# Where eight blocks of weight digits are made: all ahead of the pooling groups, two to every three gate steps

## The chip, the cores and the metric

The kernel runs on one core of one Trainium2 chip. The metric is the device time of one execution in microseconds (us). Before the change three executions took 1553.84, 1555.45 and 1555.94 us, a median of 1555.45 us. One more execution was profiled. It took 1551.45 us, and its span from the first to the last instruction is 1549.5 us.

The engines are named as in the profile: PE is the matrix engine and PEld its weight load, DVE the vector engine, ACT the scalar engine, POOL the GpSimd engine, SP the engine that issues most DMAs. Each takes its instructions strictly in the order in which they stand in its queue, so an instruction that waits holds up all that stand behind it.

## The reference: what is computed

One encoder layer on 1024 tokens of 1024 channels, all in float32:

```python
h = rmsnorm(x, g_mix[l])
z = h @ w_in[l]
...
y_pool = pool_mixer(u_pool, w_pool_grp[l], pool_scale[l])
...
y_attn = diff_attention(q, k, v, g_q[l], g_k[l], lam, g_sub[l], lambda_init)

gates = jax.nn.sigmoid(h @ w_gate[l] + b_gate[l])
merged = (gates[..., :D_MODEL] * (y_pool @ w_branch_pool[l])
          + gates[..., D_MODEL:] * (y_attn @ w_branch_attn[l]))
x = x + merged @ w_out[l]
h2 = rmsnorm(x, g_ffn[l])
x = x + jnp.square(jax.nn.relu(h2 @ w_up[l])) @ w_down[l]
```

The attention has eight heads with two softmax maps each. The pooling mixer has four groups of 128 channels with trailing windows of 2, 4, 8 and 16 tokens. The change touches how `w_branch_attn` is prepared for the product `y_attn @ w_branch_attn`.

## The kernel before, in words

**Products.** Every float32 product is made of three products of reduced parts (`mm3`, lines 125 to 127): a number is split into a high part, which ACT rounds (L119), and a low part, the rest, which DVE or POOL subtracts (L120). Most PE time is in these three lines.

**The attention stage** works through 8 heads of 8 token tiles each, 64 steps, as a pipeline whose stages lie some steps apart (`O`): A projects a tile to q, k and v (tile `z`), B scales them (`ms`, `qn`), C transposes (`tk`), D makes scores and softmax (`sc`, `s`), E transposes the probabilities (`ta`), F multiplies with the values (`po`), H and R make the norms (`SS`, `r`, `trr`). The weights of the next head are loaded and split during the last steps of a head; POOL makes their low parts (`wqkv`). POOL also makes every power (`ms`, L234) and scales `qn` (L433). The last tile of a head has the longest rows of probabilities, 1024 wide, and needs the most of DVE.

**The filling work.** Behind this pipeline in the program, but meant to run in its gaps on PE, stands work that the attention doesn't need:

- *Gate steps* (`gate_step`). `gates()` yields 32 steps, half a column of gate weights each: 24 matmuls of 512 columns into tile `g`, one ACT instruction (`go`, L731) and a store to DRAM. The weights of a column are loaded (L657) and split, the low part by POOL (`fwgate`). 13 gate steps come first (`G_FIRST`).
- *Four pooling groups* (`pool_group(0)` to `(3)`). For each half of the tokens: 24 matmuls (`u`), an ACT copy into tile `u` (L696), 1, 2, 3 or 4 shifted additions on DVE (L705), a scaled difference (L714), a split (`mix`), a gate step, and three matmuls (`yp`). So each group holds two gate steps.
- *Eight units of weight digits* (`weight_unit`, called by `prepare_weights`). The attention branch uses a fast matrix product with seven combinations of blocks of `w_branch_attn`. A unit loads a block (tile `wq`, two DMAs, L753), and POOL makes from it seven pairs of digits: seven roundings (L762), seven subtractions (L763), four sums or differences (L767, L779). SP stores each pair to DRAM (`wa_dram`, L764, seven DMAs). POOL alone computes here; PE, DVE and ACT take no part.

**Shared room.** A unit's block `wq` lies in the same buffer as the groups' `mix` (tag `mx`), and its digits `wd` in the same buffer as the groups' `u` (tag `fu`), and there is one of each. So a group's copy into `u` can't be made before the stores of the unit that holds the buffer have finished, and the other way round. PSUM has one bank for the filling work (`ps_f`, `N_F` = 1): while `u` waits there to be copied, no gate step can begin. Later gate steps (`G_Z` = 13 and on) take turns with the two banks of `z` as well.

**Where the units stand.** `gate_step` counts the steps, and after the steps numbered in `PREP_AT` a unit follows: before the change at steps 3, 5, 7, 9 and 12. The other three stand after the groups 0, 1 and 2. A unit may not be issued before the low part of the last weights that were split (`tc.issue_after(stored["lo"])`).

**The order.** Nobody writes the order of the queues by hand. A scheduler takes the instructions by their place in the program as a priority, and by its own estimate of when each can run, and places the filling work in the gaps of the attention that it expects. On the chip the queues are then fixed.

**After the attention stage** the remaining gate steps run, then the pooling branch (`bp`), for which `ypT` is loaded and split and whose weights `wbp` POOL splits, then the attention branch (`baX`, `baY`), which loads the digits back (`wa`, L876) and needs the norm factors that go through `r` (POOL, L594 and L595), `trr` (PE, L597) and DRAM. Then come the output projection and the MLP.

Of the kernel before, what the change touches and what calls it, by code (L numbers as in the profile page):

```python
# [36 lines left out]
N_YU = 5  # L37
N_QKVW = 8 * H
N_AHEAD_B, N_AHEAD_A = 5, 3
PREP_AT = (3, 5, 7, 9, 12)  # L40


START = "x0 g n0 w0 w1 w2u w3u x1 s0p s1 x2 s2p s3 x3"
# [14 lines left out]
def encoder_kernel(  # L58
# [688 lines left out]
    def weight_unit(src, digits, kk, ch):  # L747

        cs = slice(ch * 256, (ch + 1) * 256)
        q = fq.tile([P, 4, 256], F32, tag="mx", name=f"wq{kk}_{ch}")  # L750
        for i in range(2):
            r0 = (kk + 4 * i) * P
            nc.sync.dma_start(  # L753
                q[:, i::2, :], src[r0 : r0 + P, :].rearrange("p (i c) -> p i c", i=2)[:, :, cs]
            )
        a11, a12, a21, a22 = (q[:, i, :] for i in range(4))
        buf = fu_tile(f"wd{kk}_{ch}").rearrange("p (s h c) -> p s h c", s=2, h=2)

        def put(j, a):
            d = buf[:, nput[0] % 2]  # L760
            nput[0] += 1
            nc.gpsimd.tensor_copy(d[:, 0, :].bitcast(F32R), a)  # L762
            nc.gpsimd.tensor_tensor(d[:, 1, :].bitcast(F32R), a, d[:, 0, :], op=ALU.subtract)  # L763
            nc.sync.dma_start(digits[ORDER_BA.index((j, kk))][:, :, cs], d)  # L764

        def minus(o, x_, y_):
            nc.gpsimd.tensor_tensor(o, x_, y_, op=ALU.subtract)  # L767

        nput = [0]
        put("1", a11)  # L770
        minus(a21, a11, a21)
        put("7", a21)
        put("2", a12)
        minus(a21, a22, a21)
        put("6", a21)
        put("4", a22)
        minus(a12, a12, a21)
        put("3", a12)
        nc.gpsimd.tensor_tensor(a11, a11, a21, op=ALU.add)  # L779
        put("5", a11)  # L780
# [5 lines left out]
    def gate_step():  # L786
        more = next(gate_units, "end") != "end"
        steps[0] += 1
        if steps[0] in PREP_AT:
            prepare_weights()  # L790
        return more

    def prepare_weights():
        with tc.issue_after(stored["lo"]):
            weight_unit(w_branch_attn, wa_dram, *units_left.pop(0))
# [3 lines left out]
    for g in range(4):  # L799
        for _ in pool_group(g):  # L800
            gate_step()
        if g < 3:
            prepare_weights()
    while gate_step():
        pass
    assert not units_left
# [648 lines left out]
```

## Time and profile before

| what | value |
|---|---|
| median of three executions | 1555.45 us |
| the profiled execution, its own time | 1551.45 us |
| its span | 1549.5 us |
| PE busy | 1519.3 us, 98% of the span |
| DVE busy | 1052.1 us, 68% |
| ACT busy | 814.5 us, 53% |
| POOL busy | 361.0 us, 23% |
| clock granted to PE | 1.00 |

The profiled execution is 4.0 us below the median of the others. The attention stage lies between about 15 and 690 us of the span, the branch products end at about 840, the MLP takes the rest. In the windows below, a stretch's length less its PE busy time is the time in which PE had nothing running; matmuls are pipelined, so a matmul's own duration is longer than the distance to the next one.

### The profile page before, as it was taken

The numbers are of one execution on the slowest core, as the hardware profiler recorded it, in microseconds if no ns is written. First come the engines' busy times: TensorE is split into PE (matmuls) and PEld (weight loads), VectorE is DVE, ScalarE is ACT, GpSimd is POOL, SyncE is SP. The second block draws the span as 40 slices with busy tenths as digits, with TensorE's granted clock in tenths as the row PEclk, the third lists the DMA queues.
The fourth block names the chain that finished last, engine by engine and source line by source line (L and its number), as shares of the span: only waits on it lengthen the run. The fifth ranks groups of instructions, "written<-read, shape, count | busy, mean of one in ns | idle before, by whom it ended". The sixth has DMA issues, their size and how long they took to land.

```text
span 1549.5 us, 22331 instructions
## 1 busy us (share of the span) xinstructions
PE 1519.3 (98%) x7601; PEld 1309.8 (85%) x7601; DVE 1052.1 (68%) x2349; ACT 814.5 (53%) x1808; POOL 361.0 (23%) x536
## 2 busy tenths in 40 slices
PE   7999999999999999999999999999999999999998
PEld 6999999989889899788888887888888788888887
DVE  6777777777877787843568648766666668556672
ACT  6666565556565655544454556556555634333331
POOL 6666572434636373312000000000000000000000
PEclk9999999999999999999999999999999999999999
DMA  7343331111213141627675733555443789537650
GB/s 243 119 128 102 99 110 42 56 54 62 89 40 126 37 137 48 213 76 237 249 258 178 264 109 121 182 170 181 134 139 109 254 310 397 193 123 249 230 193 27
DMA packets 183275, 235.80 MB, mean 152 GB/s; under 512 B 11685, under 2 KB 114810, under 8 KB 183162
## 3 DMA queue, kind: packets, MB, share of 16 engines
q1 hardware_dynamic: 165754, 207.08, 40.3%
q10 hardware_dynamic: 17408, 27.30, 4.7%
q8 instruction: 60, 0.98, 0.3%
q14 instruction: 53, 0.43, 0.1%
HBM read 165.10 MB, written 69.24 MB: 151 GB/s over the span
## 4 chain that ended last, share of the span: by engine, by line
PE 84%; DVE 6%; DMA 3%; issue 3%; ACT 2%; SPq 1%; POOL 0%; POOLq 0%; ACTq 0%; DVEq 0%
PE z L125 5%; PE z L127 5%; PE z L126 5%; PE Da L126 4%; PE Da L127 4%; PE Da L125 4%; PE g L125 3%; PE g L126 3%; PE g L127 3%; PE Db L126 3%; PE Db L127 3%; PE Db L125 3%; PE X L125 2%; PE X L127 2%; PE X L126 2%
## 5 line engine op out<-in xcount | busy, mean ns | idle before, releaser
L125 PE MATMUL z<-wqkv,hT 128*128 128x384 f32 x512 | 174.7, 342 | 0.8 <-DVE qn L427 0.7
L127 PE MATMUL z<-wqkv,hT 128*128 128x384 f32 x512 | 173.3, 339 | 0.0
L126 PE MATMUL z<-wqkv,hT 128*128 128x384 f32 x512 | 173.1, 339 | 0.0
L496 ACT ACTIVATE s<-s,nm 128x256 f32<-128x256 f32 (+7 forms) x128 | 99.7, 779 | 70.9 <-DVE nm L488 67.0
L125 PE MATMUL g<-hT,fwgate 128*128 128x512 f32 x256 | 101.0, 394 | 0.7 <-ACT go L731 0.5
L125 PEld LDWEIGHTS z<-wqkv,hT 128*128 128x128 f32 x512 | 96.5, 188 | 5.1 <-DVE qn L427 2.5
L126 PE MATMUL g<-hT,fwgate 128*128 128x512 f32 x256 | 100.7, 393 | 0.0
L127 PE MATMUL g<-hT,fwgate 128*128 128x512 f32 x256 | 100.2, 393 | 0.0
L126 PEld LDWEIGHTS z<-wqkv,hT 128*128 128x128 f32 x512 | 96.5, 189 | 2.7 <-POOL wqkv L120 0.2
L127 PEld LDWEIGHTS z<-wqkv,hT 128*128 128x128 f32 x512 | 96.3, 188 | 2.5 <-DVE hT L120 0.7
L234 POOL TENSOR_TENSOR ms<-ms,mhalf 128x4 f32<-128x4 f32 x64 | 67.0, 1046 | 96.2 <-DVE ms L233 79.4
L488 DVE CUSTOM_DVE_ANT_0 s<-sc,dist 128x512 f32<-128x512 f32 (+3 forms) x128 | 74.6, 584 | 17.6 <-PE sc L486 16.1
L485 PE MATMUL sc<-K,Q 128*128 128x512 f32 (+2 forms) x192 | 67.5, 361 | 2.1 <-DVE nm L488 1.9
L120 DVE TENSOR_TENSOR AS<-s,AS 128x512 fp32r<-128x512 f32 x64 | 43.8, 687 | 35.5 <-ACT AS L119 35.3
L486 PE MATMUL sc<-K,Q 128*128 128x512 f32 (+2 forms) x192 | 66.0, 354 | 0.0
L120 POOL TENSOR_TENSOR wqkv<-rqkv,wqkv 128x384 fp32r<-128x384 f32 x60 | 63.2, 1068 | 11.8 <-ACT wqkv L119 8.5
L459 ACT CAST Q<-tk 64x128 fp32r<-64x128 f32 x128 | 33.2, 260 | 61.1 <-DVE Q L458 58.8
L120 POOL TENSOR_TENSOR fwgate<-frgate,fwgate 128x512 fp32r<-128x512 f32 x32 | 43.4, 1361 | 87.4 <-ACT fwgate L119 78.8
L456 ACT CAST Q<-tk 64x128 fp32r<-64x128 f32 x128 | 33.0, 258 | 44.9 <-DVE K L455 43.5
L125 PEld LDWEIGHTS g<-hT,fwgate 128*128 128x128 f32 x256 | 48.1, 188 | 9.9 <-ACT go L731 1.1
L127 PEld LDWEIGHTS g<-hT,fwgate 128*128 128x128 f32 x256 | 48.0, 188 | 8.7
L126 PEld LDWEIGHTS g<-hT,fwgate 128*128 128x128 f32 x256 | 48.1, 188 | 8.0
(460 smaller groups left out, 4652.7 us busy)
## 6 DMA issues: line engine op xcount, KB each, us to landing
wd<-in_w_down_dram SPq DMA_DIRECT2D x56, 512.0 KB, 5.6
wu<-in_w_up_dram SPq DMA_DIRECT2D x32, 512.0 KB, 4.8
udS<-us SPq DMA_DIRECT2D x64, 256.0 KB, 2.7
ur<-udS SPq DMA_DIRECT2D x32, 512.0 KB, 3.4
wa_dram<-wd SPq DMA_DIRECT2D x56, 256.0 KB, 2.8
wa<-wa_dram SPq DMA_DIRECT2D x28, 512.0 KB, 6.5
rqkv<-in_w_in_dram SPq DMA_DIRECT2D x64, 192.0 KB, 2.7
ud<-u ACTq DMA_DIRECT2D x48, 256.0 KB, 2.1
```

Source lines behind the costliest of these rows:

```text
L120: return (lo_eng or nc.vector).tensor_tensor(lo, src, f(hi), op=ALU.subtract)
L125: nc.tensor.matmul(ps, lhs_hi, rhs_hi, start=first, stop=False, **kw)
L126: nc.tensor.matmul(ps, lhs_hi, rhs_lo, start=False, stop=False, **kw)
L127: nc.tensor.matmul(ps, lhs_lo, rhs_hi, start=False, stop=last, **kw)
L234: nc.gpsimd.tensor_tensor(dst, dst, mhalf[:, :n], op=ALU.pow)
L456: nc.scalar.copy(q_hi, q)
L459: nc.scalar.copy(Q[other, m, 1, :], q)
L485: nc.tensor.matmul(dst, Q[:, i, 0, :], rhs, start=True, stop=False)
L486: nc.tensor.matmul(dst, Q[:, i, 1, :], rhs, start=False, stop=True)
L488: nc.vector.tensor_tensor_reduce(out=s[i][:, c : c + w], in0=sc[:, 0:w], in1=dist[:, o0 + c : o0 + c + w], scale=2.0 ** -(h + 1), scalar=B ...
L496: nc.scalar.activation(s[i][:, 0:n], s[i][:, 0:n], AF.Exp, bias=last, scale=-1.0, accum_out=Z[:, i, t : t + 1])
```

## The change

All eight units now follow gate steps: two to every three steps, after the steps 2, 3, 5, 6, 8, 9, 11 and 12. None is left between the groups. Nothing is computed otherwise; the number of instructions of each kind stays.

```diff
-PREP_AT = (3, 5, 7, 9, 12)
+PREP_AT = (2, 3, 5, 6, 8, 9, 11, 12)
...
     for g in range(4):
         for _ in pool_group(g):
             gate_step()
-        if g < 3:
-            prepare_weights()
     while gate_step():
         pass
```

The scheduler makes new queues from this. Three places of them follow.

The first is SP's queue around the loads of group 1. `frpool` and `rgrp` are loads of a pooling group's weights, `frgate` of a gate column's, `rqkv` of the next head's, `wq` is the load of a unit and `wa_dram<-wd` are its stores. Before:

```order
L657 DMA frpool_1_7914<-in_w_in_dram 128x4x128
L690 DMA rgrp_7919<-in_w_pool_grp_dram 128x128
L657 DMA frgate_0_8034<-in_w_gate_dram 128x4x128
L753 DMA wq_1_7880<-in_w_branch_attn_dram 128x2x256 x2
L657 DMA frgate_1_8039<-in_w_gate_dram 128x4x128
L764 DMA wa_dram<-wd_1_7883 256x1x256
L308 DMA rqkv_2_4224<-in_w_in_dram 128x3x128 x2
L308 DMA rqkv_3_4233<-in_w_in_dram 128x3x128 x2
L764 DMA wa_dram<-wd_1_7883 256x1x256
L308 DMA rqkv_0_5045<-in_w_in_dram 128x3x128 x2
L308 DMA rqkv_1_5054<-in_w_in_dram 128x3x128 x2
L764 DMA wa_dram<-wd_1_7883 256x1x256 x5
```

The same group's loads in SP's queue after the change:

```order
L657 DMA frpool_0_7967<-in_w_in_dram 128x4x128
L657 DMA frpool_1_7972<-in_w_in_dram 128x4x128
L690 DMA rgrp_7977<-in_w_pool_grp_dram 128x128
L657 DMA frgate_0_8092<-in_w_gate_dram 128x4x128
L657 DMA frgate_1_8097<-in_w_gate_dram 128x4x128
L308 DMA rqkv_2_4224<-in_w_in_dram 128x3x128 x2
L308 DMA rqkv_3_4233<-in_w_in_dram 128x3x128 x2
L308 DMA rqkv_0_5045<-in_w_in_dram 128x3x128 x2
L308 DMA rqkv_1_5054<-in_w_in_dram 128x3x128 x2
```

The load and the seven stores of the sixth unit have left this place, and now stand ahead of the loads of group 0. Those of the seventh and the eighth, which stood at the groups 2 and 3, now stand among the loads of group 0 and end ahead of those of group 1.

The second place is DVE's queue at the end of head 5 (the sixth of eight). `s_7` and `cf_7` belong to its last tile, `rz` marks its norms; `sum` and `mix` are group 2's first half. Before:

```order
L705 TENSOR_TENSOR sum_0_4_8156<-sum_0_2_8153 128x508
L457 TENSOR_TENSOR Q_0_5432<-tk_0_5429,Q_0_5432 64x128
L458 TENSOR_TENSOR Q_0_5432<-tk_0_5429,Q_0_5432 64x128
L711 TENSOR_TENSOR sum_0_4_8156<-sum_0_4_8156,inv 128x7
L714 SCALAR_TENSOR_TENSOR sum_0_4_8156<-sum_0_4_8156,u_8123 128x505
L712 TENSOR_TENSOR sum_0_4_8156<-sum_0_4_8156,u_8123 128x7
L590 RECIPROCAL rz_5846<-Z_4423 128x8
L455 TENSOR_TENSOR K_0_5258<-tk_0_5429,K_0_5258 64x128
L120 TENSOR_TENSOR AT_3_0l<-ta_6_0_5458,AT_3_0h 128x4x128
L488 ISA s_7_1_5446,nm_7_5447<-sc_7_1_0_5481,dist 128x512
L488 ISA nm_7_5447 128x1
L120 TENSOR_TENSOR mix_0_8162<-sum_0_4_8156,mix_0_8162 128x512
```

The same place after the change:

```order
L457 TENSOR_TENSOR Q_0_5432<-tk_0_5429,Q_0_5432 64x128
L458 TENSOR_TENSOR Q_0_5432<-tk_0_5429,Q_0_5432 64x128
L590 RECIPROCAL rz_5846<-Z_4423 128x8
L455 TENSOR_TENSOR K_0_5258<-tk_0_5429,K_0_5258 64x128
L120 TENSOR_TENSOR AT_3_0l<-ta_6_0_5458,AT_3_0h 128x4x128
L120 TENSOR_TENSOR oqs_2_5517<-oq_2_5513,oqs_2_5517 128x256
L457 TENSOR_TENSOR Q_0_5432<-tk_0_5429,Q_0_5432 64x128
L458 TENSOR_TENSOR Q_0_5432<-tk_0_5429,Q_0_5432 64x128
L488 ISA s_7_1_5446,nm_7_5447<-sc_7_1_0_5481,dist 128x512
L488 ISA nm_7_5447 128x1
```

Group 2's first half has moved out of the end of head 5, to the middle of the head, and its second half begins nine rows behind the last tile's L505. Group 3's second half, which stood in the last head, now stands at the end of head 6, where its first half stood.

The third place is POOL's queue at the end of the attention stage. `fwgate` are the last gate columns, `wbp` weights of the pooling branch, `r` the norm factors of the last head, which `trr` on PE waits for. Before:

```order
L120 TENSOR_TENSOR fwgate_0_8761<-frgate_0_8759,fwgate_0_8761 128x512
L120 TENSOR_TENSOR fwgate_1_8766<-frgate_1_8764,fwgate_1_8766 128x512
L594 TENSOR_TENSOR r_7119<-r_7119,mhalf 128x8
L595 TENSOR_TENSOR r_7119<-r_7119,rz_7118 128x8
L120 TENSOR_TENSOR wbp_0_8942<-rbp_8940,wbp_0_8942 128x512
L120 TENSOR_TENSOR wbp_1_8945<-rbp_8940,wbp_1_8945 128x512
L120 TENSOR_TENSOR wbp_0_9038<-rbp_9036,wbp_0_9038 128x512
```

After the change:

```order
L120 TENSOR_TENSOR fwgate_0_8761<-frgate_0_8759,fwgate_0_8761 128x512
L120 TENSOR_TENSOR fwgate_1_8766<-frgate_1_8764,fwgate_1_8766 128x512
L120 TENSOR_TENSOR wbp_0_8942<-rbp_8940,wbp_0_8942 128x512
L120 TENSOR_TENSOR wbp_1_8945<-rbp_8940,wbp_1_8945 128x512
L594 TENSOR_TENSOR r_7119<-r_7119,mhalf 128x8
L120 TENSOR_TENSOR wbp_0_9038<-rbp_9036,wbp_0_9038 128x512
L595 TENSOR_TENSOR r_7119<-r_7119,rz_7118 128x8
```

The last head's factors now stand behind three splits of the pooling branch's weights. On PE, `trr` stood 43 gate matmuls ahead of the first `bp`; it now stands behind the first 23 matmuls of `bp`. And of the filling matmuls (`g`, `u`, `yp`) 295 stood behind the beginning of the last `z` tile before, and 242 do now: the scheduler has placed 53 more of them among the heads before.

## The prediction

> **What bounds the kernel now.** I read the page first, then the waits of PE, then windows around each stretch in which PE had nothing running. The page:
>
> ```profile
> span 1549.5 us, 22331 instructions
> ...
> PE 1519.3 (98%) x7601; PEld 1309.8 (85%) x7601; DVE 1052.1 (68%) x2349; ACT 814.5 (53%) x1808; POOL 361.0 (23%) x536
> ...
> PE   7999999999999999999999999999999999999998
> ...
> POOL 6666572434636373312000000000000000000000
> ...
> PE 84%; DVE 6%; DMA 3%; issue 3%; ACT 2%; SPq 1%; POOL 0%; POOLq 0%; ACTq 0%; DVEq 0%
> ```
>
> PE is busy 98% of the span and holds 84% of the chain that ended last. The change takes no matmul away, so it can only gain or lose in PE's gaps, 1549.5 - 1519.3 = 30.2 us in all. POOL, which makes the units, works in the first half only and is on that chain with 0%. A unit costs POOL this (columns: nanoseconds shortest/median/longest):
>
> ```profile
> L762 POOL CAST wd<-wq x56: 388/398/1171, 43.6 to 580.6; 128x256 fp32r<-128x256 f32 x56
> L763 POOL TENSOR_TENSOR wd<-wq,wd x56: 724/737/1612, 44.7 to 581.4; 128x256 fp32r<-128x256 f32 x56
> L767 POOL TENSOR_TENSOR wq<-wq x24: 722/737/1290, 35.8 to 573.5; 128x256 f32<-128x256 f32 x24
> ...
> L779 POOL TENSOR_TENSOR wq<-wq x8: 729/739/741, 47.0 to 572.4; 128x256 f32<-128x256 f32 x8
> ```
>
> Seven of the first, seven of the second, three and one of the others: 7 x 0.398 + 7 x 0.737 + 4 x 0.737 = 10.9 us of POOL for each of the three units that move. Where PE's gaps are, the windows show (length, then busy us and instructions of PE, PEld, DVE, ACT, POOL):
>
> ```profile
> 50.00:125.00 75.00, 75.00 (x433) 69.58 (x432) 58.74 (x189) 46.08 (x138) 53.31 (x85) 1.00 0.40 129
> 125.00:300.00 175.00, 174.60 (x1026) 161.64 (x1025) 127.77 (x428) 106.14 (x314) 84.17 (x123) 1.00 0.25 80
> ...
> 388.70:418.00 29.30, 27.29 (x159) 24.49 (x158) 25.26 (x84) 18.28 (x53) 19.21 (x33) 1.00 0.31 100
> 432.60:438.00 5.40, 3.26 (x19) 2.39 (x18) 4.84 (x16) 3.65 (x10) 3.00 (x4) 1.00 0.37 119
> 488.70:502.90 14.20, 14.20 (x87) 13.47 (x86) 11.26 (x39) 7.38 (x22) 6.92 (x11) 1.00 0.23 81
> 512.00:520.00 8.00, 6.62 (x41) 5.76 (x40) 6.43 (x24) 5.34 (x15) 2.40 (x3) 1.00 0.21 72
> 570.60:590.60 20.00, 20.00 (x124) 19.34 (x122) 16.08 (x49) 10.10 (x29) 12.47 (x23) 1.00 0.25 86
> 590.60:600.00 9.40, 8.65 (x46) 7.19 (x46) 8.51 (x26) 5.26 (x13) 4.03 (x4) 1.00 0.10 29
> 625.00:675.00 50.00, 46.75 (x234) 37.77 (x233) 40.42 (x101) 25.11 (x64) 10.96 (x17) 1.00 0.46 158
> 750.00:775.00 25.00, 25.00 (x112) 20.68 (x112) 13.03 (x21) 11.25 (x19) 0.00 (x0) 1.00 0.60 224
> ```
>
> PE's gaps, length less busy: 2.01 us in 388.7 to 418, 2.14 at 433, 1.38 at 516, 0.75 at 597 and 3.25 in 625 to 675. Together 9.53 us can be won here; the rest lies in the start, the MLP and small change. The last row gives a price: 112 matmuls of 512 columns in 25 us, 0.223 us each.
>
> **Part by part.** *The units between the groups go.* The stretch from 388.7 is the one behind unit 6:
>
> ```profile
> 388.50 0.40 PE L127 MATMUL u<-hT,fwpool 128*128 128x512 f32 x1
> ...
> 412.70 0.61 ACT L696 COPY u<-u 128x512 f32<-128x512 f32 x1
> ...
> 417.95 0.39 PE L125 MATMUL g<-hT,fwgate 128*128 128x512 f32 x1
> ```
>
> Group 1's matmuls end at 388.9, but their copy out of the one bank waits 24 us for the room that unit 6's stores still read; only then can the next filling matmul come, at 417.95. For 29 us PE lives on the attention alone, with DVE busy 25.26 of 29.30 us, and 2.01 us are lost. Behind units 7 and 8 (488.7 to 502.9 and 570.6 to 590.6) the same hole costs 0.00 us: the queued attention filled PE there. I take 1.5 of the 2.01 us as won (bounds 0 and 2.01, since the attention may be late at this place for DVE's sake).
>
> The hole doesn't vanish: unit 8 now stands right ahead of group 0, whose `u` must wait for its stores. The three holes cost 2.01, 0.00 and 0.00 us, so I add their mean, 0.7 (bounds 0 and 2.01).
>
> *The groups come earlier against the heads.* At 433 and 516 a head ends: DVE has its widest rows and PE waits for it.
>
> ```profile
> 401.32 0.17 DVE L233 TENSOR_SCALAR ms<-ms 128x4 f32<-128x4 f32 x1
> ...
> 433.57 1.28 DVE L505 SCALAR_TENSOR_TENSOR s<-s,cf,s 128x1024 f32<-128x1024 f32 x1
> ...
> 434.97 1.03 DVE L233 TENSOR_SCALAR ms<-ms 128x4 f32<-128x4 f32 x1
> ...
> 434.54 1.43 POOL L120 TENSOR_TENSOR fwgate<-frgate,fwgate 128x512 fp32r<-128x512 f32 x1 [9.71 <-ACT fwgate L119]
> ...
> 436.61 0.63 PE L541 MATMUL ta<-identf,s 128*128 128x128 f32 x4 [1.65 <-DVE AT_4l L120]
> ```
>
> PE waits 1.65 us for `AT_4l`, which stands behind these DVE rows. At 433 `yp` of group 1 and a late gate split fall on this point; at 516 four wide instructions of group 2 stand just ahead of it on DVE (the order shows them). After the change group 1's and 2's first halves lie in the middle of their heads. I take 1.6 of 2.14 and 1.0 of 1.38 as won (bounds 0 and all of each), because PE has only 0.40 us of gaps in 125 to 300, where two head ends have no group on them.
>
> At 597, group 3's first half stands on the head's end and costs 0.75 us; after the change its second half stands there, as many wide instructions. I count 0 (from 0.75 won to 1.4 lost, the difference to the gap at 433). In the last head that second half is gone from 628 to 635, where DVE was busy 40.42 of 50 us; the norm factors' loads and products (`ry`) stay. Of 3.25 us I take 1.8 as won (0 to 3.25).
>
> *Three more units in the front.* In 50 to 125 three units already run, with POOL busy 53.31 of 75 us, and PE has no gap at all. In 125 to 300 there were two; with three more POOL goes from 84.17 to 84.17 + 3 x 10.9 = 116.9 of 175 us, 67%, below the 71% of the first stretch. Cover is the same attention work, so I add 0.2 (0 to 2.0, what one hole cost). SP's loads of the next head's weights pass between unit stores there, as they did in 50 to 125.
>
> The 1.03 us above for an instruction that takes 0.17 us elsewhere lies beside a running POOL split. [...]
>
> *The end of the attention.* 53 fewer filling matmuls, 53 x 0.223 = 11.8 us, stand behind the beginning of the last tile, so the last head's own waits have less cover. What must be in time:
>
> ```profile
> 696.38 0.28 PE L576 MATMUL po<-oqs,ones 128*128 128x256 f32 x1
> ...
> 700.39 1.64 POOL L594 TENSOR_TENSOR r<-r,mhalf 128x8 f32<-128x8 f32 x1 [1.84 <-DVE r L593]
> ...
> 702.10 0.54 POOL L595 TENSOR_TENSOR r<-r,rz 128x8 f32<-128x8 f32 x1
> ...
> 705.02 0.27 PE L597 MATMUL trr<-identf,r 128*8 128x128 f32 x1
> ...
> 711.41 1.14 ACT L119 CAST ypT<-rypT 128x512 fp32r<-128x512 f32 x2 [1.77 <-DMA rypT<-p_dram]
> ...
> 714.92 0.39 PE L125 MATMUL bp<-ypT,wbp 128*128 128x512 f32 x1
> ...
> 716.85 3.79 POOL L120 TENSOR_TENSOR wbp<-rbp,wbp 128x512 fp32r<-128x512 f32 x3 [14.21 <-ACT wbp L119]
> ```
>
> Before, `trr` stood 9.9 us ahead of `bp`; now it stands 23 x 0.223 = 5.1 us behind its start, and POOL makes two `wbp` splits, `r`, a third split and the product with `rz` for it. On ACT the casts of `ypT` now stand ahead of the last `oqs`, on which the sums at 696.38 wait. ACT's queue was held before by the last head's own `oq` until PE had finished, which it no longer is at that point, so the loads should come earlier too. I add 0.8 (0 to 6.2, worked out at the first rival).
>
> The sum: -1.5 + 0.7 - 1.6 - 1.0 + 0 - 1.8 + 0.2 + 0.8 = -4.2 us. Against the profiled execution's own time of 1551.45 us that is 1547.25. The median of the runs lies 4.0 us higher, at 1555.45, so the forecast is 1551.2 us. What a measurement of this kernel can tell from no change is about 0.2%, 3.1 us.
>
> **The rivals.**
>
> *The end runs dry: slower.* Suppose `ypT` and `wbp` come where they came before, against the start of `bp`. The last `ypT` cast ended at 712.55, 2.4 us ahead of `bp`. Behind it now follow about 1.6 us of ACT and DVE work for `oqs` (four instructions of about 0.4 us each), so the sums can run 0.8 us ahead of `bp`, but stand 19 matmuls, 4.2 us, ahead: 3.4 us of waiting. The third split ended at 720.64; with `r` and the product, 1.64 + 0.54 us, `trr` could come 7.9 us after `bp` (720.64 + 2.18 - 714.92), against 5.1: 2.8 more. That makes 6.2 us, and the 1.8 us at this place aren't won: -1.5 + 0.7 - 1.6 - 1.0 + 0.2 + 6.2 = +3.0, 1558.5 us; with all of the lost 11.8 us of cover, 1564. It decides from 3.2 us of waiting on. For it speaks the order; against it that the trace shows ACT standing idle before the casts for loads which the earlier groups can bring forward. Chance 0.15.
>
> *The gaps only change place: same.* The scheduler has moved nearly every filling matmul; where new neighbours wait, as the 2.14 us at 433 came by a chance meeting, the 9.53 us of gaps return elsewhere. 1555.5 us. For it speaks that the gaps have several causes, against it the 0.40 us in 175 us where no group was. Chance 0.18.
>
> *Each unit takes its delay along: same.* If it is the unit's work beside DVE, not the waiting copy, that costs 2.01 us, three units in the front cost 6.0 in place of my 0.2: -4.2 - 0.2 + 6.0 = +1.6, 1557.1 us. Against it: 50 to 125 with three units and no gap. Chance 0.12.
>
> That the change doesn't do what it says is excluded by the order, which shows the units ahead of group 1.
>
> **How the numbers follow.** Forecast (faster by over 0.2%, below 1552.3 us): 0.55. Within 0.2%: 0.18 + 0.12 = 0.30. Slower: 0.15. The lowest end takes all 9.53 us as won and no price paid: 1555.45 - 9.5 = 1545.9. The highest is the first rival's 1558.5; beyond it lie its own worse cases. Range 1546.0 to 1558.5.
>
> **What would show it.** Right: a group's copy (L696) within about 4 us of its last `u` matmul for groups 1 to 3; PE gaps under 1 us at the ends of the heads 4 and 5; no new gap in 125 to 300. Wrong: PE waits before `po<-oqs,ones` or `trr` of more than 3 us, a gap of over 1 us per unit in the front, or gaps in 300 to 700 that still sum to 9 us.

## The result and the profile after

The changed kernel took 1548.64 us (median of 8 executions, 1546.07 to 1553.24), the kernel before 1555.26 us (8 executions, 1551.19 to 1556.55). The ratio is 0.9952, 95% interval 0.9936 to 0.9968: faster by 0.5%. On a second chip session, below, it was 0.9952 again. The forecast was 1551.2 us in a range of 1546.0 to 1558.5.

The profiled execution of the changed kernel took 1548.64 us, with a span of 1546.9 us. Its page, in the parts that were shown of before:

```profile
span 1546.9 us, 22321 instructions
...
PE 1518.9 (98%) x7601; PEld 1313.5 (85%) x7601; DVE 1055.0 (68%) x2349; ACT 816.9 (53%) x1808; POOL 360.8 (23%) x536
...
POOL 6668777334334252312000000000000000000000
...
PE 84%; DVE 5%; DMA 4%; ACT 3%; issue 2%; SPq 1%; POOL 0%; POOLq 0%; ACTq 0%; DVEq 0%
```

POOL's row shows the move. Against before's row, slices 4, 5 and 7 (116 to 193 and 232 to 271 us) are fuller, and slices 11 and 13 to 16 (387 to 425 and 464 to 619 us) are emptier. The windows at the places of the prediction, with the same columns:

```profile
50.00:125.00 75.00, 75.00 (x433) 69.53 (x432) 58.36 (x188) 46.11 (x138) 53.73 (x85) 1.00 0.40 129
125.00:300.00 175.00, 175.00 (x1028) 162.52 (x1027) 128.71 (x425) 106.65 (x311) 115.47 (x175) 1.00 0.38 121
388.70:418.00 29.30, 28.26 (x160) 25.19 (x159) 24.05 (x76) 16.37 (x46) 10.84 (x16) 1.00 0.22 68
432.60:438.00 5.40, 5.40 (x33) 4.98 (x33) 4.81 (x17) 2.62 (x9) 1.23 (x2) 1.00 0.00 0
488.00:491.00 3.00, 1.36 (x6) 0.72 (x5) 2.56 (x8) 2.60 (x10) 0.87 (x1) 1.00 0.00 0
491.00:493.00 2.00, 2.00 (x8) 1.83 (x8) 1.93 (x9) 2.00 (x5) 0.82 (x2) 0.59 0.30 111
493.00:495.00 2.00, 2.00 (x8) 2.00 (x8) 1.93 (x9) 1.33 (x4) 1.28 (x2) 0.55 0.23 86
512.00:520.00 8.00, 8.00 (x47) 7.32 (x45) 5.08 (x15) 4.84 (x14) 1.29 (x1) 1.00 0.08 25
590.60:600.00 9.40, 9.40 (x55) 8.72 (x54) 7.40 (x23) 5.66 (x16) 3.32 (x5) 1.00 0.24 70
625.00:675.00 50.00, 48.65 (x257) 41.63 (x256) 38.71 (x109) 26.10 (x71) 15.44 (x18) 1.00 0.45 159
```

PE's gaps at 433, 516 and 597 are gone; 1.04 us are left in 388.7 to 418 and 1.35 us in 625 to 675. A gap of 1.64 us is new at 488 to 491, and behind it the granted clock (the column before the DMA share) is 0.59 and 0.55 in two windows of 2 us; the trace's own record of the clock has 0.50 for 3.41 us there. The timeline of PE and ACT at this gap:

```profile
488.43 0.40 PE L127 MATMUL g<-hT,fwgate 128*128 128x512 f32 x1
...
489.66 0.33 PE L541 MATMUL ta<-identf,s 128*128 128x128 f32 x1 [0.83 <-DVE AT_0l L120]
...
490.80 0.47 PE L485 MATMUL sc<-K,Q 128*128 128x512 f32 x1 [0.82 <-ACT Q L456]
...
491.20 0.69 ACT L731 ACTIVATE go<-g,cols 128x512 f32<-128x512 f32 x1
```

A gate step ends at 488.43 us, and the next filling matmul comes only at 497.68 us. In between PE lives on the attention alone, as it did behind a waiting copy, though no copy of a group waits here.

Group 1's first copy, in the timeline around 390 us:

```profile
390.12 0.39 PE L127 MATMUL u<-hT,fwpool 128*128 128x512 f32 x1
391.35 0.56 ACT L696 COPY u<-u 128x512 f32<-128x512 f32 x1
...
393.52 0.39 PE L125 MATMUL g<-hT,fwgate 128*128 128x512 f32 x1
```

The copy comes 1.2 us behind the last `u` matmul, where it came 24.2 us behind it before, and the next filling matmul 3.4 us behind, in place of 29.5 us. None of the eight copies waits over 2.1 us.

**A finer measure.** A busy time hides part of each gap: a 512-column matmul is on record for 0.39 us, but the next one begins 0.227 us after it, so 0.16 us of each gap count as busy. In what follows, *lost time* is worked out from the start of every matmul: the distance to the next start, less the steady pitch of its form (0.2265 us for 512 columns, 0.173 for 384, 0.117 for 256, 0.108 for 128). It holds the gaps in full, and the stretches at a lower clock. In us, with each kernel's two profiled executions (the second ones are among the experiments):

```
stretch       25-300  300-388  388-418  418-450  450-505  505-530  530-610  610-700  700-930  930-end
before          5.96     2.94     4.17     3.01     1.06     1.90     2.09     6.35     0.66     7.57
before, 2nd     5.48     2.53     4.96     3.06     1.47     1.96     2.12     5.00     1.30     7.64
after           4.48     2.36     2.25     0.42     4.31     1.29     1.18     2.91     3.03    10.22
after, 2nd      4.80     2.45     2.31     0.42     4.26     1.31     1.18     2.66     2.09    11.43
```

From 25 to 700 us the loss falls from 27.5 and 26.6 to 19.2 and 19.4 us, about 7.7 us. Behind 700 us 4.8 us come back. The two rows of a kernel differ by less than 1.0 us in every stretch but two (1.35 us at 610 to 700 of before, 1.21 us behind 930 of after). So where a kernel's gaps lie goes for the most part with its order; single gaps, and stretches at half clock, come and go.

Two places lose part of what the attention won. At 703 us PE waits for `oqs` of the last head (timeline; the bracket names what ended the wait):

```profile
699.56 1.14 ACT L119 CAST ypT<-rypT 128x512 fp32r<-128x512 f32 x2 [2.71 <-DMA rypT<-p_dram]
...
702.58 1.14 ACT L119 CAST ypT<-rypT 128x512 fp32r<-128x512 f32 x2 [1.88 <-DMA rypT<-p_dram]
...
703.63 0.37 ACT L565 ACTIVATE oq<-po 128x256 f32<-128x256 f32 x1
...
704.62 0.39 PE L576 MATMUL po<-oqs,ones 128*128 128x256 f32 x1 [1.52 <-ACT oqs L119]
```

`oq` could have run at about 697 us; it stood behind casts that waited for their loads. The other place is the MLP, which shares nothing with the units. Its first row here is before's, the others are after's:

```profile
960.54 0.50 PE L125 MATMUL W<-BT4h,A 128*128 128x512 f32 x1 [0.92 <-ACT A L119]
```

```profile
956.88 0.50 PE L125 MATMUL X<-BT3h,AS 128*128 128x512 f32 x1 [2.19 <-ACT AS L119]
...
1231.32 0.50 PE L125 MATMUL X<-BT3h,AS 128*128 128x512 f32 x1 [2.08 <-ACT U L1211]
```

In the new queues the product `X` of `BT3` stands ahead of the product `W`, and PE loses 2.35 us in place of 1.09 us there (by starts: 956.88 less the start before it, 954.30, less the pitch). Behind the gap that ends at 1231 us the clock was halved for 3.4 us in both profiled executions of after and in neither of before, another 1.6 us. In the second of after it was also halved behind the gap at 956 us.

### The profile page after: what moved, and what is told of

Read it like the earlier page. It is cut to its first block, busy times and chain, and to the rows that moved or that the text cites. A ratio compares the mean times of both kernels' runs of the same rounds, so it can differ in the third digit from the quotient of the medians.

```text
span 1546.9 us, 22321 instructions
## 1 busy us (share of the span) xinstructions
PE 1518.9 (98%) x7601; PEld 1313.5 (85%) x7601; DVE 1055.0 (68%) x2349; ACT 816.9 (53%) x1808; POOL 360.8 (23%) x536
## 4 chain that ended last, share of the span: by engine, by line
PE 84%; DVE 5%; DMA 4%; ACT 3%; issue 2%; SPq 1%; POOL 0%; POOLq 0%; ACTq 0%; DVEq 0%
PE z L125 5%; PE z L127 5%; PE z L126 5%; PE Da L125 4%; PE Da L126 4%; PE Da L127 4%; PE Db L125 3%; PE Db L126 3%; PE Db L127 3%; PE g L125 3%; PE g L127 3%; PE g L126 3%; PE X L125 2%; PE X L126 2%; PE X L127 2%
## 5 line engine op out<-in xcount | busy, mean ns | idle before, releaser
L120 POOL TENSOR_TENSOR fwgate<-frgate,fwgate 128x512 fp32r<-128x512 f32 x32 | 44.7, 1400 | 47.6 <-ACT fwgate L119 47.2
```

The costliest lines, as they stand in the source:

```text
L120: return (lo_eng or nc.vector).tensor_tensor(lo, src, f(hi), op=ALU.subtract)
```

## The experiments

Theory A is the waiting copy: a unit between two groups holds the room of the next group's `u`, PE has no filling work until its stores are done, and what PE loses in the attention comes from there. Theory B: a unit's POOL work delays DVE and the attention wherever it stands. Theory C: the order is new, the gaps have changed place, and the total is chance. The medians, each with its ratio to before in the same session, and what PE lost:

```
kernel         median us  ratio   95% interval      copies that waited over 4 us   25-700  700-930  930-end
own_room       1553.45    0.9984  0.9973 to 0.9995  none                             24.2      2.0     11.1
left_out       1548.57    0.9946  0.9932 to 0.9959  none                             23.6      1.3      7.2
back_0         1553.18    0.9980  0.9968 to 0.9992  15.9                             26.3      2.2     10.2
end_fixed      1549.98    0.9951  0.9936 to 0.9966  none                             19.0      2.6     11.2
before again   1555.26    0.9996  0.9981 to 1.0011  25.0, 12.2, 14.7                 26.6      1.3      7.6
after again    1548.14    0.9952  0.9934 to 0.9969  none                             19.4      2.1     11.4
pool_free      1558.15    1.0015  1.0001 to 1.0028  none                             23.7      9.2      8.3
eleven         1557.48    1.0020  1.0007 to 1.0033  44.7                             30.3      2.7      8.1
late           1554.56    0.9990  0.9978 to 1.0002  none                             17.5     11.5     11.6
own_front      1548.73    0.9947  0.9934 to 0.9960  none                             20.4      2.4     12.1
back_2         1554.83    0.9991  0.9980 to 1.0002  24.4                             30.0      1.0      9.6
late_fixed     1552.82    0.9985  0.9976 to 0.9994  none                             16.8      9.3      8.2
```

**own_room: the digits in a buffer of their own, units where they were.**

```diff
-        buf = fu_tile(f"wd{kk}_{ch}").rearrange(...)
+        buf = fd.tile([P, S], F32, tag="fd", name=f"wd{kk}_{ch}").rearrange(...)
...
-        return fp.tile([P, 576], F32, tag="fo", name=name, bufs=N_FO)
+        return fp.tile([P, 528], F32, tag="fo", name=name, bufs=N_FO)
```

> The kernel before with its three units still between the pooling groups, but with the digits `wd` in a buffer of their own, so that a group's copy into `u` no longer waits for a unit's stores (two other tiles are made smaller or shared to find the room). Theory A, the waiting copy: the copy of group 1 comes within 4 us of its last `u` matmul, the 2.0 us of PE gaps in the 29 us behind it go, the gaps at 433 and 516 too, and PE's gaps from 0 to 700 us fall from 21.0 to about 16 us: 1548 to 1551 us. Theory B, the units' POOL work beside DVE costs the time: the work stands where it stood, so 1555 us. Theory C, only the chance meetings of the filling work with the heads' ends change: anything from 1550 to 1558, with gaps of 1 to 2 us at new places.

The copy of group 1 came 1.9 us behind its last `u`, and most of the loss at 433 and 516 went (0.7 us each). But 388 to 418 lost 4.4 us as before, now by another wait: DVE's 640-column row of the softmax takes 1.59 us beside POOL's splits (0.87 us at its shortest in before), and the rows of the group stand among the attention's. These splits are not a unit's work: the sixth unit's last rounding starts at 388.1 us. The timeline there (own_room's lines are two higher):

```profile
398.76 1.59 DVE L507 SCALAR_TENSOR_TENSOR s<-s,cf,s 128x640 f32<-128x640 f32 x1
...
399.63 1.85 POOL L122 TENSOR_TENSOR fwgate<-frgate,fwgate 128x512 fp32r<-128x512 f32 x1
...
400.75 0.75 DVE L714 TENSOR_TENSOR sum<-sum,u 128x3 f32<-128x3 f32 x1
400.88 0.66 PE L543 MATMUL ta<-identf,s 128*128 128x128 f32 x4 [1.71 <-DVE AT_0l L122]
```

By busy time A's number came: PE's gaps from 0 to 700 us fell from 21.0 to 16.3 us. By the starts the attention lost 24.2 us, only 2.4 to 3.3 less than before, since 450 to 505 us now loses 5.3 us in place of 1.1 and 1.5, with 3.4 us at half clock from 496 us on. The time, 1553.45 us, lies above A's 1548 to 1551. So A holds for part of it, B is not needed for that part, and C is not out.

**left_out: the three units between the groups not made at all.**

```diff
-        if g < 3:
-            prepare_weights()
...
-        nc.sync.dma_start(f(wa), wa_dram[n])
+        j, kk = ORDER_BA[n]
+        nc.sync.dma_start(f(wa), wa_dram[ORDER_BA.index((j, kk % 2))])
```

> The kernel before without the three units between the groups; they aren't made anywhere, and the attention branch reads the blocks of the rows 0 and 1 twice instead (the output is not the reference's). Bounds what the move can win. Theory A: as the changed kernel, 1548.6 us, within 1.5 us, since three more units in the front cost nothing. Theory B: better than the changed kernel by the cost of three units in the front, at 1.0 to 2.0 us each 1543 to 1546 us. Theory C: between 1548 and 1555, by where the heads' ends meet the groups.

1548.57 us: what the changed kernel takes, with three units less. By time that is A's number. By place it isn't the same kernel: its attention loses 23.6 us, 4 more than after, and its MLP 7.2 us, 3 to 4 less, since its MLP kept before's order. Two unlike sums came out alike.

**back_0: the eighth unit back between the groups 0 and 1.**

```diff
-PREP_AT = (2, 3, 5, 6, 8, 9, 11, 12)
+PREP_AT = (2, 3, 5, 6, 8, 9, 11)
...
             gate_step()
+        if g == 0:
+            prepare_weights()
```

> The changed kernel with one unit, the eighth, back between the groups 0 and 1. Theory A: the copy of group 1 waits again for more than 15 us, PE loses 2 us in the stretch behind it and the later groups come about 5 us later: PE's gaps from 300 to 700 us are 5.4 + 2 to 4 us, and the time is 1550.5 to 1552.5 us. Theory B: one unit of work is only moved from the front to here: 1549 to 1550.6 us. Theory C: no bound to the unit's place, 1546 to 1556 us.

1553.18 us. The copy behind the unit waits 15.9 us again, and 1.9 us are lost until PE has filling work again, A's 2 us. PE's gaps by busy time from 300 to 700 us are 7.8 us, 2.4 more than after's 5.4, within A's 2 to 4. But the time lies above A's 1550.5 to 1552.5: by the starts 20.5 us are lost there against after's 14.7, most of it away from the copy (5.1 us in 300 to 388, 6.7 in 610 to 700, each with 3.4 us at half clock).

**end_fixed: the casts of `ypT2` and `ypT3` behind the last `oqs`.**

```diff
-    ypT = [load_split(p_dram, g * P, f"ypT{g}", ypt_tile) for g in range(4)]
+    ypT = [load_split(p_dram, g * P, f"ypT{g}", ypt_tile) for g in range(2)]
+    with tc.issue_after(last_o["oqs"]):
+        ypT += [load_split(p_dram, g * P, f"ypT{g}", ypt_tile) for g in (2, 3)]
```

> The changed kernel, with the casts of `ypT2` and `ypT3` on ACT held behind the last head's last `oqs`. If the 1.7 us that PE waits at 703 us for `oqs` come from ACT's queue, where `oq` stands behind casts that wait for their loads, the sums run at about 698 us and the time falls by 1.5 us, to about 1547 us. The rival: the wait is taken over by the first `bp`, which then waits for `ypT3`, or by `trr`, and the time stays at 1548.6 us.

The wait at 703 us went: `oq` ran at 695.55 us. But `baX` now waits 1.75 us, for a product `mp` that waits for its gate values. The timeline of ACT, DVE and PE there:

```profile
752.25 0.72 ACT L831 ACTIVATE g<-g,zero 128x512 f32<-128x512 f32 x1 [2.45 <-DMA g<-g_dram]
...
753.01 0.69 DVE L210 TENSOR_TENSOR mp<-bp,g 128x512 f32<-128x512 f32 x1 [2.48 <-ACT g L831]
...
753.75 0.50 PE L126 MATMUL baX<-yb,wa 128*128 128x512 f32 x1 [1.58 <-DVE mp L210]
```

The rival was right in the time, 1549.98 us, no gain, though the wait went to `baX` and not to `bp` or `trr`. One wait for a load had covered the next.

**before and after again, unchanged.**

> The kernel before, unchanged, for a second profile: the profiled execution of before took 1551.45 us, 3.4 us below the median of its runs. If that execution had luck in a place that has nothing to do with the change, the second shows about 3 us more there, in the MLP behind 930 us (7.6 us of PE's lost time in the first profile, 10 us in four others); if not, its gaps in the attention are larger, 24 us or more from 0 to 700 instead of 21.

> The changed kernel, unchanged, for a second profile: from 25 to 700 us PE loses 19 us against its steady pitch, as in the first, within 1.5 us, where before lost 27.5. If that is scatter between executions, it is 22 or more. Time 1548.6 us.

Both second profiles show the places of the first. Neither of the two expectations for before came: its MLP lost 7.6 us both times, and its gaps by busy time from 0 to 700 us were 19.8 us, less than the first's 21.0 and not 24. The second profiled execution took 1553.08 us, below its median again.

**pool_free: own_room without the POOL work of the three units.**

```diff
         def put(j, a):
+            if len(units_left) < 3:
+                nc.sync.dma_start(digits[ORDER_BA.index((j, kk))][:, :, cs], q[:, 0:2, :])
+                return
```

> The kernel with the digits in a buffer of their own (1553.5 us), with the loads and the stores of the three units between the groups, but none of their POOL instructions: pieces of the loaded block are stored as they are, so these digits are wrong. If the units' POOL work beside the attention is what the buffer of their own did not win back, the time falls to that of the kernel with the three units left out, 1548.5 to 1550 us. If it is SP's queue, in which the next head's weight loads stand among the unit's stores, or the DMA, it stays at 1552.5 to 1554 us.

Neither number came: 1558.15 us. The cause is not in the attention, which loses 23.7 us against own_room's 24.2, but in a new order at its end, where the first `bp` products wait 3.5 us and the branches lose 9.2 us in place of 2.0. For theory B the part that counts is the first: POOL was busy 330.1 us in place of own_room's 360.3, and with these 30 us taken away the attention won 0.5 us. Place by place it is no clean test, since the order is new here too: 388 to 418 and 450 to 505 lose 3.5 and 2.7 us less than in own_room, 530 to 610 loses 5.2 us more. B's price of 1 to 2 us for each unit isn't seen in the sum; a smaller one isn't excluded. In own_room's rows above, a 128x3 difference took 0.75 us, where before's differences of this line took 0.15 to 0.17, and it ended at 401.50 us, the POOL split beside it at 401.48. The prediction's row of 1.03 us, which takes 0.17 us elsewhere, ended at 436.00 us, its split at 435.97. That these splits held the rows up is a reading of two meetings; no run isolates it.

**eleven: three units more in the front.**

```diff
-PREP_AT = (2, 3, 5, 6, 8, 9, 11, 12)
+PREP_AT = (2, 3, 4, 5, 6, 7, 8, 9, 10, 11, 12)
...
-    units_left = [(kk, ch) for kk in range(4) for ch in range(2)]
+    units_left = [(kk, ch) for kk in range(4) for ch in range(2)] + [(3, 1)] * 3
```

> The changed kernel with eleven units in the front, one after each of the steps 2 to 12, the last three a repeat of the eighth. Prices the crowding of the front. If units cost nothing there, as the changed kernel against the one with three units left out says, the time stays within 1.5 us of 1548.6 us, with the groups later by some steps. If a unit costs 1 to 2 us wherever it stands, it is 1551.6 to 1554.6 us.

1557.48 us, slower than before and above both expected numbers. The front itself costs little even so: 5.96 us are lost in 25 to 300, as in before, 1.2 to 1.5 more than in after. But the last units aren't done when group 0 has its `u`, and this is the hole of the prediction at its full size (the window, then ACT's timeline):

```profile
307.60:352.50 44.90, 39.33 (x226) 35.70 (x224) 35.43 (x112) 24.87 (x73) 31.98 (x50) 0.96 0.37 118
```

```profile
352.09 0.59 ACT L696 COPY u<-u 128x512 f32<-128x512 f32 x1
```

The copy waits 44.7 us, and PE loses 10.1 us while it does.

**late: one unit after each of the steps 5 to 12.**

```diff
-PREP_AT = (2, 3, 5, 6, 8, 9, 11, 12)
+PREP_AT = (5, 6, 7, 8, 9, 10, 11, 12)
```

> The changed kernel with its eight units after the steps 5 to 12, one to each. No unit stands between the groups here either, but the filling work comes into another order: the first `u` begins with the 28th tile of the attention in place of the 30th, and the later groups come 4 to 6 tiles earlier. If the gain comes from the three places between the groups alone (theory A), the time is within 1.5 us of the changed kernel's 1548.4 us. If part of it is where the groups happen to meet the ends of the heads (theory C), it differs: PE's lost time from 25 to 700 us is not 19 but 21 to 26 us, and the time 1549 to 1556 us.

The attention loses 17.5 us, less than after's 19.2 and less than C's 21 to 26, and yet the kernel takes 1554.56 us, C's time, because the end runs dry. Of the filling matmuls 207 stand behind the beginning of the last `z` tile, in place of after's 242, and PE stands still ahead of `trr` (timeline):

```profile
723.47 1.41 DVE L198 SCALAR_TENSOR_TENSOR ry<-ry,gs,rb 128x512 f32<-128x512 f32 x2 [7.79 <-DMA ry<-y_dram]
724.80 0.28 DVE L579 CUSTOM_DVE_ANT_0 oq<-po,identf 128x128 f32<-128x128 f32 x1
...
726.47 1.64 POOL L594 TENSOR_TENSOR r<-r,mhalf 128x8 f32<-128x8 f32 x1 [19.95 <-DVE r L593]
...
729.65 0.38 PE L597 MATMUL trr<-identf,r 128*8 128x128 f32 x1 [7.08 <-POOL r L595]
```

DVE waited 7.8 us for a load of `ry`, with the last head's `r` behind it. The late `trr` is the first rival of the prediction, in another kernel, but by another wait: the rival named ACT's casts and POOL's splits, and here it is a load that DVE waits for.

**own_front: the buffer of own_room, with all units in the front** (its edit is that of own_room and of the change together).

> The kernel with the digits in a buffer of their own, and with all eight units in the front. No copy waits for a store at all, and the order of the filling work is a third one. Theory A: the changed kernel's time, 1548.4 us, within 1.5 us. Theory C: PE's lost time from 25 to 700 us between 21 and 26 us, 1549 to 1555 us. A clear win over the changed kernel, under 1546 us, would show that the front's units still held something up.

1548.73 us, A's number, and 20.4 us in the attention. A third order of the filling work, free of copy waits, gives the changed kernel's time; a buffer more gives nothing beyond it.

**back_2: the eighth unit back between the groups 2 and 3** (as back_0, with `g == 2`).

> The changed kernel with the eighth unit back between the groups 2 and 3, where the kernel before had a unit whose copy wait cost PE nothing. If each unit between groups costs by its waiting copy only where the attention can't fill PE, 1548.5 to 1550.5 us; if one costs as much as the one between the groups 0 and 1 did (1553.2 us, 4.6 us more than the changed kernel), 1552 to 1554 us.

1554.83 us, above both expected ranges. Here the copy waits 24.4 us and PE loses 5.9 us meanwhile, at a place where before lost 0.3 us in a wait of 14.7 us. What a copy wait costs depends on its length and on what of the attention falls into it.

**late_fixed: `late` with the products `ry` of the heads 6 and 7 behind the last `r` on DVE.**

```diff
-                yr[k] = y_scaled(k, row_factors(k))
+                with tc.issue_after(r_made[H - 1]):
+                    yr[k] = y_scaled(k, row_factors(k))
```

> The kernel with its units after the steps 5 to 12 (1554.6 us), with one change on DVE at the end of the attention: the products `ry` of the heads 6 and 7 stand behind the last head's norm factor `r`, where one of them stood ahead of it and waited 7.8 us for its load. PE's and POOL's orders stay as they were. If the 7.2 us that PE waits for `trr` there are this one wait, `trr` comes in time or within 0.5 us, and the clock that is granted lower for some us behind the gap goes with it: 1546 us, 1545 to 1548, 2 us less than the changed kernel. The rival: the wait passes on to the attention branch, as it did when the casts of `ypT` were moved: 1549 to 1553 us.

`trr` came in time, and the next `bp` waited instead:

```profile
721.75 0.27 PE L598 MATMUL trr<-identf,r 128*8 128x128 f32 x1
722.93 1.42 DVE L199 SCALAR_TENSOR_TENSOR ry<-ry,gs,rb 128x512 f32<-128x512 f32 x2 [4.68 <-DMA ry<-y_dram]
...
726.54 0.72 ACT L830 ACTIVATE g<-g,zero 128x512 f32<-128x512 f32 x1 [6.65 <-DMA g<-g_dram]
...
728.08 0.24 ACT L600 COPY rT<-trr 8x128 f32<-8x128 f32 x1
728.37 0.79 PE L126 MATMUL bp<-ypT,wbp 128*128 128x512 f32 x1 [6.35 <-ACT rT L600]
```

The room for the gate values `g` is held until that `ry` is made, so their load comes late, ACT waits for it, and the copy that frees `trr`'s bank stands behind on ACT. The rival was right: 1552.82 us. What binds the end in this order is the load of `ry`, and it was not made faster. No version beat the changed kernel.

**Taken together.** From 25 to 700 us every kernel with a copy wait of over 15 us loses 26.3 to 30.3 us, and every kernel without one 16.8 to 24.2 us. Among those without, the ones with all eight units in the front lose 16.8 to 20.4 us, and those with five there 23.6 to 24.2. So theory A is shown in sign: with a long copy wait the attention loses more, in every kernel. While the three copies of before waited and until PE had filling work again, it lost 4.9 and 5.7 us in the two profiles. That the waits are the cause of all of this isn't shown, since own_room, with no wait, loses as much at the first of these places; in sum own_room puts the waiting copies at about 3 us of the attention's 7.7. The remaining 4 to 5 us came with the full front and its new order of the groups. That all three orders with a full front (after, late, own_front) have it speaks against pure chance, but no run here isolates why. Theory C is right about the rest of the kernel: behind 700 us the loss went from 8.2 us (before) to 23.1 us (late), though no unit stands there in any of them.

## Why the prediction was right, and where its sizes were off

- *The bound.* PE's gaps were taken as the only thing to win. PE stayed the bound in every kernel, but a second price hangs on the gaps that stood in no term: stretches of 3.4 us at half clock behind some of them, 1.6 us each.
- *The hole behind unit 6* (-1.5 us). The copy came in time as forecast, and the size was too small: 4.2 and 5.0 us were lost there by starts, 2.3 after, so 2.3 us won. The window's 2.01 us had hidden the 0.16 us of each gap and the slower matmuls right behind it; in the second profile there were also 3.4 us at half clock from 407 us on. That the waiting copy alone made this loss isn't shown: in own_room it stayed.
- *The hole moved to group 0* (+0.7 us). It didn't come: the last store of the units has landed at 269 us, the first `u` copy is at 308 us, and 300 to 388 lost 0.3 us less. In eleven, where the units do run into group 0, it came with 10.1 us. The term belonged to a condition, whether the units are done by then, that could have been estimated.
- *The heads' ends* at 433 (-1.6), 516 (-1.0) and 597 (0). Measured -2.6, -0.6 and -0.9. But a new meeting at 488 us costs 3.0 us, half of it at half clock. "The gaps only change place" was true of this one; the rival's total wasn't.
- *The last head* (-1.8). Measured -2.9.
- *The front* (+0.2). Measured -1.1; three units cost nothing there, and by eleven six would cost 0.2 us against before. The third rival, that a unit takes its delay along at 2 us each, is out by this; the sum of pool_free speaks against it too.
- *The end* (+0.8). Measured +2.4 and +0.8 in the two pairs of profiles. Of the first rival, half came: the sums waited, 1.7 and 0.9 us, on ACT's queue as described; `trr` did not wait. late shows that PE can wait 7.2 us for `trr`, though by a load on DVE, not by the queues that the rival named.
- *The MLP* (not in the sum). +3.2 us. It was taken as untouched, since no term pointed there, while the order of the two kernels differs in it: the longer gap at 957 us costs 1.3 us more, the half-clock stretch at 1232 us 1.6 us, and in the second profile another one at 956 us.

By the profiles the sum is -7.7 in the attention, +1.6 at the end and +3.2 in the MLP: -2.9 us, where -5.0 and +0.8 had been forecast. That this sum lies near the forecast's -4.2 us is luck in part: the attention won 2.7 us more than forecast, and the end and the MLP lost 4.0 us more.

The medians moved by 6.6 us, more than either. Of the kernel before, both profiled executions (1551.45 and 1553.08 us) lie below the median of the 105 that were timed beside the experiments, 1555.8 us. The clock tells most of this, as an estimate. The medians of before's executions go from 1553.4 us at a mean granted clock of 1.000 to 1559.2 us at 0.994, about 1 us for each 0.001. The profiled ones had 1.000 and 0.998, where the median is 0.997: 2 us. Those of after had 0.998 and 0.996, where the median is 0.998: 1 us the other way. Added to the -2.9 us that makes -5.9 of the -6.6. Where the longer executions lost their time is in no trace.

## What to carry to other kernels

Two uses of one buffer can stop an engine that neither use runs on: here a store held a buffer, the buffer an ACT copy, the copy the one PSUM bank, and the bank PE's filling work (at group 1 of before the copy came 24.2 us behind the last `u` matmul, the next filling matmul 29.5 us). Such preparation belongs where its room is free until the last store is done, early enough that it doesn't run into the next user. Where an automatic scheduler makes the order, a change's far side counts too: compare the order to the program's end, and measure PE's loss from start to start rather than from busy time.

## What the runs showed of the hardware

A gap of a microsecond or two on PE can cost as much again. In after, two gaps of 1.0 us within 2.3 us, at 488 us, were followed by 3.4 us at half clock (the rows of 491 and 493 above) and 1.6 us of loss, in both its profiled executions. By the traces' records of the clock, 29 such stretches in the fourteen profiled executions, ahead of the spans' ends, last 3.41 us each. In late one of 10.24 us begins within the gap of 7.1 us before `trr`, in late_fixed one of 6.83 us within the gap of 6.4 us before `bp`: three and two times that length. The same gaps don't always do it. Before has three gaps (0.5, 0.7 and 0.75 us) between 635 and 639 us of its second profiled execution, and the same three between 633 and 637 us of its first. The window behind them in the second, and then in the first:

```profile
639.00:642.00 3.00, 3.00 (x15) 2.90 (x14) 2.42 (x6) 1.29 (x6) 0.00 (x0) 0.50 0.30 115
```

```profile
639.00:642.00 3.00, 3.00 (x15) 2.49 (x14) 2.79 (x10) 2.23 (x9) 0.00 (x0) 1.00 0.60 221
```

Gaps that come to 2.0 to 2.2 us were enough in one piece (2.08 us, up to 1231.32 us of after), in two (at 488 us) and in three (before's second execution). What decides whether such a stretch follows is not shown.

With the clock goes the executions' scatter. Of 105 timed executions of before, the 44 with a mean granted clock of 0.998 or more have a median of 1553.8 us, the 44 with 0.996 or less 1557.2 us. Of 15 executions of after 10 have 0.998 or more, with a median of 1547.4 us. At the same clock the two kernels are 6.4 us apart, and fewer executions of after fall low. That fewer gaps bring fewer such stretches would fit, but the executions behind it have no trace, so it is argued and not shown. The profiled ones don't bear it out: ahead of the end of the span, before has none and two such stretches, after two and three.
